# Sums of squares at two changes of layer: vector adds replaced by products with ones

## The chip, the cores and the metric

The kernel runs on one core of a Trainium2 chip. Its time is the device time of one execution in microseconds (us): 3379.16 us, the median of three runs (3367.13, 3379.16 and 3380.83). TensorE (PE) does the matrix products, VectorE (DVE), ScalarE (ACT) and GpSimd (POOL) the elementwise work, SyncE (SP) issues the transfers. Each engine executes its own list of instructions strictly in order, and semaphores tie the lists together.

## What is computed

Two blocks, each two layers deep, over 512 tokens of width 1024, in fp32. The first block has six sublayers (feed-forward, mixer, feed-forward, twice), each between two RMS norms. The second block works on the 512 tokens and on 256 context tokens together: an even layer (a gated recurrence called rwkv, beside a Fourier mix), then an odd layer (retention). What matters here is the frame around every sublayer:

```python
def rmsnorm(x, g):
    xf = x.astype(jnp.float32)
    y = xf * lax.rsqrt(jnp.mean(xf * xf, axis=-1, keepdims=True) + EPS)
    return (y * g.astype(jnp.float32)).astype(x.dtype)

def _sublayer(x, fn, pre_g, post_g, shift, scale, gate, res_w):
    h = _rmsnorm(x, pre_g) * (1.0 + scale[:, None, :]) + shift[:, None, :]
    y = _rmsnorm(fn(h), post_g)
    return x + res_w * (1.0 + gate[:, None, :]) * y
```

So after each sublayer the new x = x + gate*norm(y) is squared, summed over the 1024 features of a token, and the inverse root of that mean scales x for the next sublayer.

## The kernel before

The width lies on the partitions, so x is eight tiles x0 to x7 of 128 features by 512 tokens, and a sum over features is a sum over eight tiles and 128 partitions. `residual` (L389) does the end of a sublayer for one half of 256 tokens: it takes the inverse roots of y (`rstd_bc`, L331: products `st_ps<-ones,yacc`, a square root on ACT, a reciprocal on DVE, and products `bc<-cst,r` that spread the result over all partitions), scales y on DVE, adds it to x on POOL (L402), and squares the new x on ACT. Then there are two ways to the sum. Between the sublayers of block 1 (`boundary`, L416) PE takes for each tile two products `xs<-ones,sq` of one column each, called a pair below; they accumulate over the eight tiles in PSUM. At the two changes of layer (end of block 1 into `even_layer`, and `even_layer` into the odd layer) DVE adds the eight squares into a tile (`sumsq`, L355: `xacc`, `xcacc`, `xkeep`), and only the next layer's `norm_in` (L903) makes products, root, reciprocal and `bc` of it. `norm_in` then computes the split input of the next layer, tile by tile: `hf` on DVE, the high part on ACT, the low part on DVE (`ehh`/`ehl` in the even layer; `oc` for the context, `oh`/`ol` for the tokens in the odd layer).

Every large product is made of three (high by high, high by low, low by high; `acc3`, L270). A weight tile arrives as `raw`, ACT makes its high part `whi`, DVE its low part `wlo`.

In the even layer's recurrence twelve slots follow each other, two per pair of heads. Slots of one kind, called d=0 slots below, carry projections of the context (`ipc`, 24 products of 256 columns) and of the tokens (`ipm`, 24 of 512) as filler beside a chain: DVE solves small triangular systems (`un`), SP moves them through DRAM (`ad<-un`, `blocks<-ad`), DVE transposes them (`tn<-blocks`), and PE and ACT make the block inverse (`p<-tn,am`, `g<-p`, `p<-g,blocks`, `p<-tn,am`, `p<-g,up`). `ipm` has a single PSUM buffer, which ACT frees by reading it (`u<-ipm`). On ACT stand there also the decays (`DC<-L`, `F<-L`, `L<-L`, exponentials of the scans `L` that DVE makes) and a square root `hr<-hst`, which needs another function table and so a table load on each side.

Nothing of the order is written by hand here: a scheduler simulates the program as a whole and writes out one list per engine, so that a change in one place can move instructions elsewhere.

Of the kernel before, what the change touches and what calls it, by code (L numbers as in the profile page):

```python
# [8 lines left out]
F32 = mybir.dt.float32  # L9
F32R = mybir.dt.float32r  # L10
AF = mybir.ActivationFunctionType
# [3 lines left out]
D = 1024  # L15
KD = 8
T = 512
# [131 lines left out]
class K:  # L149
# [236 lines left out]
        self.act(y[o][:, cols], ps[:, cols], AF.Copy)  # L386
        self.sumsq(yacc, ps[:, cols], o == 0, cols)

    def residual(self, x, y, yacc, c0, n, G, xacc=None, last=False):  # L389

        cols = slice(c0, c0 + n)
        bc = self.rstd_bc(yacc, c0, n, 1.0 / D, self.eps6)
        gates = list(zip(self.PEG, self.stats))
        sums = [self.paux("xs", *self.NST) for _ in range(2)] if xacc is None and not last else []
        done = None
        for k in range(KD + 1):
            if k < KD:
                with self.tc.issue_after(done.ins) if done and not self.POOLX else nullcontext():
                    self.stt(y[k][:, cols], y[k][:, cols], G[:, k : k + 1], bc[:, cols])
            if k:  # L400
                new = x[k - 1][:, cols]
                done = (self.nc.vector if last and k % 2 == 0 and (c0 or k > 4) else self.nc.gpsimd).tensor_tensor(out=new, in0=new, in1=y[k - 1][:, cols], op=ALU.add)  # L402
                if xacc is not None:
                    self.sumsq(xacc, new, k == 1, cols)
                elif last:
                    self.nc.sync.dma_start(self.A["out"][k - 1][:, cols], new)
                else:
                    sq = self.tp.tile([128, n], F32, tag=f"sq{n}", name="sq", bufs=self.NSQ)
                    self.act(sq, new, AF.Square)
                    for i, ps in enumerate(sums):  # L410
                        m = self.mm(ps[:, :1], sq[:, 128 * i : 128 * i + 128], self.ones, k == 1, k == KD)
                    gates.append((self.XEG[0] + int(self.XEG[1] * k), m))
        self.pe_gates = [] if last else gates
        return [ps[:, :1] for ps in sums]

    def boundary(self, x, out, G, nxt):  # L416
# [363 lines left out]
    def block1(self, stages, after):  # L780
# [75 lines left out]
        for i, (l, s) in enumerate(order):  # L856
# [25 lines left out]
            if i + 1 < len(order):  # L882
                hs = self.boundary(self.x, out, G, nxt)
            else:
                self.xacc = self.xp.tile([128, 512], F32, tag="xacc", name="xacc")
                for c0, n in self.HALVES:
                    self.residual(self.x, *next(out), c0, n, G(), self.xacc)


    def ada2(self, l, mods):  # L890
# [12 lines left out]
    def norm_in(self, src, acc, g1, shift, hs, c0, halves):  # L903

        for o, n in halves:
            cols, dst = slice(o, o + n), slice(c0 + o, c0 + o + n)
            bc = self.rstd_bc(acc, o, n, 1.0 / D, self.eps6)
            for k in range(KD):
                t = self.t("hf")
                self.stt(t[:, cols], src[k][:, cols], g1[:, k : k + 1], bc[:, cols])  # L910
                hi, lo = hs[k]
                self.act(hi[:, dst], t[:, cols], AF.Identity, bias=shift[:, k : k + 1])
                self.stt(lo[:, dst], t[:, cols], shift[:, k : k + 1], hi.bitcast(F32)[:, dst], ALU.add, ALU.subtract)
# [20 lines left out]
    def even_layer(self):  # L934
# [8 lines left out]
        with tc.tile_pool(name="exc", bufs=1, reuse_waits="tile") as p:  # L943
            self.tp, self.NT = p, 4
            xc = self.load_ctx(p)
            cacc = p.tile([128, TC], F32, name="cacc")
            for k in range(KD):
                self.sumsq(cacc, xc[k], k == 0, slice(0, TC))
            self.norm_in(xc, cacc, g1c, mods["shiftc"], hs, 0, ((0, TC),))
            self.norm_in(self.x, self.xacc, g1l, mods["shiftl"], hs, TC, self.HALVES)  # L950
        xd = self.dp.tile([KD, 128, T], F32, name="xd")
        for k in range(KD):
            nc.sync.dma_start(xd[k], self.x[k])
# [11 lines left out]
        with tc.tile_pool(name="eo", bufs=1, reuse_waits="tile") as p:  # L965
# [4 lines left out]
            y.append(p.tile([128, CT], F32, name="oy"))  # L970
            yc, y = [t[:, :TC] for t in y], [t[:, TC:] for t in y]
            self.out_late(ins, y, yc, yacc, cacc, late, begun)
            self.xcacc = self.xp.tile([128, TC], F32, name="xcacc")
            self.residual(xc, yc, cacc, 0, TC, self.gated("Gc", mods["gatec"], 0, "Gc"), self.xcacc)
            self.xacc = self.xp.tile([128, T], F32, name="xkeep")
            G = self.gated("Gl", mods["gatel"], 0, "G")
            for c0, n in self.HALVES:
                self.residual(self.x, y, yacc, c0, n, G, self.xacc)
        ez_cm.__exit__(None, None, None)
        eh_cm.__exit__(None, None, None)  # L980
        self.xc = xc
# [690 lines left out]
    def odd_layer(self):  # L1672
# [11 lines left out]
        for k in range(KD):  # L1684
            t = self.s(f"oc{k}", F32R)
            hc.append((t[:, :TC], t[:, TC:]))
        self.norm_in(self.xc, self.xcacc, g1c, mods["shiftc"], hc, 0, ((0, TC),))
        self.norm_in(self.x, self.xacc, g1l, mods["shiftl"], hs, 0, self.HALVES)
        con = self.sp.tile([128, OCON.n], F32, name="ocon")
        nc.sync.dma_start(con, A["ocon"])  # L1690
        C = lambda name, n: con[:, OCON.at[name] : OCON.at[name] + n]
# [213 lines left out]
    def program(self, first=True, second=True, stages=6):  # L1905
        nc, tc, A = self.nc, self.tc, self.A
        self.setup()
        with self.phase({"mm": ("mm", 4), "st": ("st", 2), "bc": ("bc", 2)}, (1024, self.NWS[0]), (4, 1), self.NSS):
# [6 lines left out]
            else:  # L1915
# [1 line left out]
                self.flush()  # L1917
                self.open_x()
                self.load_x()
                self.xacc = self.xp.tile([128, 512], F32, tag="xacc", name="xacc")  # L1920
                for k in range(KD):
                    self.sumsq(self.xacc, self.x[k], k == 0, slice(0, T))
        if second:
            with self.phase({"mm": self.INV, "st": ("seq", 1), "bc": ("y", 1)}, (512, self.NWS[1]), None):
                self.even_layer()
# [111 lines left out]
```

## Time and profile before

| | |
|---|---|
| median of three runs | 3379.16 us |
| profiled execution | 3377.71 us |
| its span | 3376.0 us |
| PE busy | 3165.4 us (94%) |
| DVE busy | 1834.4 us (54%) |
| ACT busy | 1189.2 us (35%) |
| POOL busy | 287.1 us (9%) |

The span is what the profile sees of an execution; 1.7 us of the execution's time lie outside it. PE is busy nearly throughout, and the places where it is not are the changes of sublayer and of layer and parts of the recurrence. A busy PE can run at half its clock; the profile gives the granted clock of any stretch (1.00 is 2.4 GHz, 0.50 is 1.2 GHz).

### The profile page before, as it was taken

Reading aid. Unit: us, or ns where it says so; the run is one execution under the profiler, and the core shown is the slowest. Engines: PE = TensorE matmul, PEld = TensorE weight load, DVE = VectorE, ACT = ScalarE, POOL = GpSimd, SP = SyncE. Lnnn points to the kernel's source line nnn. Section 1 sums busy time; section 2 is a strip of 40 time slices with the busy share of each in tenths; the row PEclk is TensorE's granted clock in tenths of the full one; section 3 lists DMA queues with packets and bytes.
Section 4 is the critical chain, followed back from the end, with each engine's and each line's share of the span. In section 5 each row is a group of like instructions: output and inputs, shape, how many; then the busy total and the mean of one; then the engine's idle time right before and its main releaser. Section 6 shows DMA issues by size and latency. Waiting matters only on the chain. (4 is left out here: it accounts for less than half of the span.)

```text
span 3376.0 us, 58396 instructions
## 1 busy us (share of the span) xinstructions
PE 3165.4 (94%) x24530; PEld 2646.8 (78%) x24530; DVE 1834.4 (54%) x3336; ACT 1189.2 (35%) x1925; POOL 287.1 (9%) x285
## 2 busy tenths in 40 slices
PE   5999999999999999999999979999898899869998
PEld 4877887888889888878887868788787778758766
DVE  8554378444425554364667456456655655462554
ACT  4222244432223222344322234233332432242553
POOL 3000020200002000111000010011101111020000
PEclk8999999999999999999999989999999999979999
DMA  6555421144433554332355521211110111222112
GB/s 238 191 181 178 134 82 44 51 145 143 131 96 120 185 176 164 121 102 78 117 182 182 163 87 46 72 31 38 32 30 22 29 58 30 59 67 63 62 39 69
DMA packets 156503, 340.90 MB, mean 101 GB/s; under 512 B 52816, under 2 KB 64848, under 8 KB 156112
## 3 DMA queue, kind: packets, MB, share of 16 engines
q1 hardware_dynamic: 156240, 337.18, 30.8%
q8 instruction: 192, 3.15, 0.4%
q14 instruction: 71, 0.58, 0.1%
HBM read 328.20 MB, written 8.91 MB: 100 GB/s over the span
## 5 line engine op out<-in xcount | busy, mean ns | idle before, releaser
L169 ACT ACTIVATE whi<-raw 128x1024 fp32r<-128x1024 f32 (+2 forms) x451 | 426.0, 947 | 1122.1 <-PE po L174 266.4
L253 DVE TENSOR_TENSOR wlo<-raw,whi 128x1024 fp32r<-128x1024 f32 (+2 forms) x432 | 471.3, 1093 | 539.7 <-ACT whi L169 528.8
L313 DVE CUSTOM_DVE_ANT_0 raw_a<-raw_a,cond 128x1024 f32<-128x1024 f32 x176 | 215.4, 1230 | 339.2 <-DMA raw_a<-in_ada_w_dram 339.1
L174 PE MATMUL pu<-hh,whi 128*128 128x512 f32 (+1 forms) x824 | 317.5, 385 | 5.0 <-ACT whi L169 5.0
L174 PE MATMUL pu<-hh,wlo 128*128 128x512 f32 (+1 forms) x824 | 316.5, 384 | 2.9 <-DVE wlo L253 2.9
L174 PE MATMUL pu<-hl,whi 128*128 128x512 f32 (+1 forms) x824 | 316.2, 384 | 0.0
L174 PE MATMUL pg<-hh,whi 128*128 128x512 f32 (+1 forms) x752 | 293.6, 391 | 22.1 <-ACT hh L169 20.0
L174 PE MATMUL po<-ah,whi 128*128 128x512 f32 (+1 forms) x880 | 309.7, 352 | 3.0 <-ACT sq L169 3.0
L174 PE MATMUL po<-ah,wlo 128*128 128x512 f32 (+1 forms) x880 | 308.7, 351 | 0.0
L174 PE MATMUL po<-al,whi 128*128 128x512 f32 (+1 forms) x880 | 308.0, 350 | 0.0
L174 PE MATMUL pg<-hl,whi 128*128 128x512 f32 (+1 forms) x752 | 291.9, 389 | 5.2 <-DVE hl L188 5.2
L174 PE MATMUL pg<-hh,wlo 128*128 128x512 f32 (+1 forms) x752 | 292.3, 389 | 4.4 <-DVE wlo L253 4.2
L402 POOL TENSOR_TENSOR x<-x,y 128x256 f32<-128x256 f32 x106 | 77.2, 763 | 2107.7 <-DVE y L188 2107.4
L174 PEld LDWEIGHTS pg<-hh,whi 128*128 128x128 f32 x752 | 147.1, 196 | 53.7 <-ACT hh L169 22.2
L174 PEld LDWEIGHTS pu<-hh,whi 128*128 128x128 f32 x824 | 159.0, 193 | 37.4 <-ACT whi L169 5.8
L174 PEld LDWEIGHTS po<-ah,whi 128*128 128x128 f32 x880 | 166.2, 189 | 27.5 <-ACT sq L169 3.8
L174 PEld LDWEIGHTS pu<-hh,wlo 128*128 128x128 f32 x824 | 158.2, 192 | 36.1 <-DVE wlo L253 4.5
L174 PEld LDWEIGHTS po<-al,whi 128*128 128x128 f32 x880 | 166.2, 189 | 23.5
L174 PEld LDWEIGHTS po<-ah,wlo 128*128 128x128 f32 x880 | 166.2, 189 | 23.3
L174 PEld LDWEIGHTS pu<-hl,whi 128*128 128x128 f32 x824 | 158.6, 193 | 31.9
L174 PEld LDWEIGHTS pg<-hh,wlo 128*128 128x128 f32 x752 | 146.3, 195 | 37.5 <-DVE wlo L253 8.4
L174 PEld LDWEIGHTS pg<-hl,whi 128*128 128x128 f32 x752 | 146.0, 194 | 36.0 <-DVE hl L188 6.7
(468 smaller groups left out, 6507.5 us busy)
## 6 DMA issues: line engine op xcount, KB each, us to landing
raw<-in_w_dram SPq DMA_DIRECT2D x232, 512.0 KB, 4.1
raw_a<-in_ada_w_dram SPq DMA_DIRECT2D x176, 512.0 KB, 3.7
raw<-in_ev_in_dram SPq DMA_DIRECT2D x60, 256.0 KB, 2.6
raw<-in_w_dram SPq DMA_DIRECT2D x32, 384.0 KB, 3.6
raw_a<-in_ada_w_dram SPq DMA_DIRECT2D x32, 256.0 KB, 5.6
raw<-in_ab_in_dram SPq DMA_DIRECT2D x16, 512.0 KB, 3.2
raw<-in_ev_out_dram SPq DMA_DIRECT2D x20, 256.0 KB, 2.7
raw<-in_w_dram SPq DMA_DIRECT2D x16, 256.0 KB, 2.6
```

The source lines that it names most:

```text
L169: ins = self.nc.scalar.activation(out=out, in_=in_, func=func, scale=scale, bias=bias)
L174: self.last_mm = self.nc.tensor.matmul(out, lhsT=lhsT, rhs=rhs, start=start, stop=stop)
L253: (self.nc.gpsimd if self.nwt <= self.POOLW else self.nc.vector).tensor_tensor(out=lo, in0=src, in1=hi.bitcast(F32), op=ALU.subtract)
L313: self.nc.vector.tensor_tensor_reduce(out=out, in0=raw, in1=v, scale=1.0, scalar=0.0, op0=ALU.mult, op1=ALU.add, accum_out=dst[:, o : o + 1])
L402: done = (self.nc.vector if last and k % 2 == 0 and (c0 or k > 4) else self.nc.gpsimd).tensor_tensor(out=new, in0=new, in1=y[k - 1][:, col ...
```

## The change

At both changes of layer `residual` now makes the sums the way `boundary` does, with pairs on PE, and it keeps the inverse roots themselves: ACT takes each square root straight from PSUM into a column of a small tile (`xrs`, four columns of 128 tokens each; `xcrs`, two columns for the context), DVE inverts them in place, and `norm_in` only spreads them (`bc<-cst,xrs`).

```diff
-    def residual(self, x, y, yacc, c0, n, G, xacc=None, last=False):
+    def residual(self, x, y, yacc, c0, n, G, keep=None, last=False):
...
-        sums = [self.paux("xs", *self.NST) for _ in range(2)] if xacc is None and not last else []
+        sums = [] if last else [self.paux("xs", *(self.NST if keep is None else self.NMM)) for _ in range(2)]
...
-                if xacc is not None:
-                    self.sumsq(xacc, new, k == 1, cols)
-                elif last:
+                if last:
                     self.nc.sync.dma_start(self.A["out"][k - 1][:, cols], new)
                 else:
                     sq = self.tp.tile([128, n], F32, tag=f"sq{n}", name="sq", bufs=self.NSQ)
                     self.act(sq, new, AF.Square)
                     for i, ps in enumerate(sums):
                         m = self.mm(ps[:, :1], sq[:, 128 * i : 128 * i + 128], self.ones, k == 1, k == KD)
-                    gates.append((self.XEG[0] + int(self.XEG[1] * k), m))
+                    if keep is None:
+                        gates.append((self.XEG[0] + int(self.XEG[1] * k), m))
         self.pe_gates = [] if last else gates
+        if keep is not None:
+            for i, ps in enumerate(sums):
+                self.act(keep[:, i : i + 1], ps[:, :1], AF.Sqrt, scale=1.0 / D, bias=self.eps6)
+            self.nc.vector.reciprocal(out=keep, in_=keep)
...
-                self.xacc = self.xp.tile([128, 512], F32, tag="xacc", name="xacc")
+                self.xrs = self.xp.tile([128, 4], F32, name="xrs")
                 for c0, n in self.HALVES:
-                    self.residual(self.x, *next(out), c0, n, G(), self.xacc)
+                    self.residual(self.x, *next(out), c0, n, G(), self.xrs[:, c0 // 128 : (c0 + n) // 128])
...
-            bc = self.rstd_bc(acc, o, n, 1.0 / D, self.eps6)
+            if isinstance(acc, tuple):
+                bc = self.paux("bc", *self.NBC)
+                for c in range(o, o + n, 128):
+                    self.mm(bc[:, c : c + 128], acc[0][:, c // 128 : c // 128 + 1].to_broadcast([128, 128]), self.con("ident", 128))
+            else:
+                bc = self.rstd_bc(acc, o, n, 1.0 / D, self.eps6)
...
-            self.xcacc = self.xp.tile([128, TC], F32, name="xcacc")
-            self.residual(xc, yc, cacc, 0, TC, self.gated("Gc", mods["gatec"], 0, "Gc"), self.xcacc)
-            self.xacc = self.xp.tile([128, T], F32, name="xkeep")
+            self.xcrs = self.xp.tile([128, 2], F32, name="xcrs")
+            self.residual(xc, yc, cacc, 0, TC, self.gated("Gc", mods["gatec"], 0, "Gc"), self.xcrs)
+            self.xrs = self.xp.tile([128, 4], F32, name="xrs")
             G = self.gated("Gl", mods["gatel"], 0, "G")
             for c0, n in self.HALVES:
-                self.residual(self.x, y, yacc, c0, n, G, self.xacc)
+                self.residual(self.x, y, yacc, c0, n, G, self.xrs[:, c0 // 128 : (c0 + n) // 128])
```

The lists of the engines differ at the two changes of layer and in three slots of the recurrence between them.

First place, the first change of layer, PE, before: the products `po` of the last feed-forward's second half, while the first half's residual runs on the other engines (numbers tell tiles of one name apart).

```order
L174 MATMUL po<-ah_13417,whi 128x256
L174 MATMUL po<-al_13418,whi 128x256
L174 MATMUL po<-ah_13417,wlo 128x256
L174 MATMUL po<-ah_13498,whi 128x256
L174 MATMUL po<-al_13499,whi 128x256
L174 MATMUL po<-ah_13498,wlo 128x256
```

The same place after the change:

```order
L174 MATMUL po<-ah_13417,whi 128x256
L174 MATMUL xs<-ones,sq 128x1 x2
L174 MATMUL po<-al_13418,whi 128x256
L174 MATMUL po<-ah_13417,wlo 128x256
L174 MATMUL xs<-ones,sq 128x1 x2
L174 MATMUL po<-ah_13498,whi 128x256
L174 MATMUL po<-al_13499,whi 128x256
L174 MATMUL xs<-ones,sq 128x1 x2
L174 MATMUL po<-ah_13498,wlo 128x256
L174 MATMUL po<-ah_13577,whi 128x256
```

Eight pairs of `xs` (each `x2`) now stand between these `po` products; the pairs of the second half follow after the last `po`.

Second place, the second change of layer, PE, before: from the norms of y to the first product of the odd layer (`pv`).

```order
L174 MATMUL st_ps<-ones,yacc 128x1 x2
L174 MATMUL bc<-cst,r 128x128 x2
L174 MATMUL st_ps<-ones,yacc 128x1 x2
L174 MATMUL bc<-cst,r 128x128 x4
L174 MATMUL st_ps<-ones,xcacc 128x1 x2
L174 MATMUL bc<-cst,r 128x128 x2
L174 MATMUL st_ps<-ones,xkeep 128x1 x2
L174 MATMUL bc<-cst,r 128x128 x2
L174 MATMUL st_ps<-ones,xkeep 128x1 x2
L174 MATMUL bc<-cst,r 128x128 x2
L174 MATMUL pv<-whi,oh_26715 128x512
```

After the change, the same stretch:

```order
L174 MATMUL st_ps<-ones,yacc 128x1 x2
L174 MATMUL bc<-cst,r 128x128 x2
L174 MATMUL st_ps<-ones,yacc 128x1 x2
L174 MATMUL xs<-ones,sq 128x1 x6
L174 MATMUL bc<-cst,r 128x128 x2
L174 MATMUL xs<-ones,sq 128x1 x14
L174 MATMUL bc<-cst,r 128x128 x2
L174 MATMUL xs<-ones,sq 128x1 x28
L174 MATMUL bc<-cst,xcrs 128x128 x2
L174 MATMUL bc<-cst,xrs 128x128 x4
L174 MATMUL pv<-whi,oh_26778 128x512
```

The `st_ps` products on `xcacc` and `xkeep` are gone, 24 pairs stand in three groups between the `bc` products of y, and all `bc` of the next layer stand behind the last pair.

The same place on DVE, before (`oy` is y, scaled; `hf` opens the next layer's norm):

```order
L188 SCALAR_TENSOR_TENSOR oy<-oy,Gl,bc 128x256 x2
L183 TENSOR_TENSOR xkeep<-xkeep,sq 128x256
L188 SCALAR_TENSOR_TENSOR oy<-oy,Gl,bc 128x256 x6
L183 TENSOR_TENSOR xkeep<-xkeep,sq 128x256 x5
L348 RECIPROCAL r<-r 128x2
L183 TENSOR_TENSOR xkeep<-xkeep,sq 128x256 x4
L188 SCALAR_TENSOR_TENSOR hf<-xc_26342,g1c,bc 128x256
L188 SCALAR_TENSOR_TENSOR hf<-xc_26343,g1c,bc 128x256
L188 SCALAR_TENSOR_TENSOR hf<-xc_26344,g1c,bc 128x256
```

After the change:

```order
L348 RECIPROCAL r<-r 128x2
L188 SCALAR_TENSOR_TENSOR oy<-oy,Gl,bc 128x256 x8
L416 RECIPROCAL xcrs<-xcrs 128x2
L188 SCALAR_TENSOR_TENSOR oy<-oy,Gl,bc 128x256 x8
L416 RECIPROCAL xrs<-xrs 128x2 x2
L188 SCALAR_TENSOR_TENSOR hf<-xc_26360,g1c,bc 128x256
L188 SCALAR_TENSOR_TENSOR hf<-xc_26361,g1c,bc 128x256
```

The 21 adds are gone, and the context's first `hf` stands behind the reciprocals of all six columns.

Third place, a d=0 slot of the recurrence (the second of the three that differ), ACT, before:

```order
L169 ACTIVATE kd<-alm,a0h 128x512
L169 ACTIVATE whi<-raw 128x512
L169 ACTIVATE u<-ipm 128x512
L169 ACT_TABLE_LOAD
L169 ACTIVATE hr<-hst 128x12
L169 ACT_TABLE_LOAD
L169 ACTIVATE DC<-L 128x12
L169 ACTIVATE F<-L 128x12x64
L169 ACTIVATE r<-u,omu 128x768
L169 ACTIVATE rt<-hr 128x768
L169 ACTIVATE L<-L 128x768
L169 ACTIVATE whi<-raw 128x512 x2
```

After the change:

```order
L169 ACTIVATE kd<-alm,a0h 128x512
L169 ACTIVATE DC<-L 128x12
L169 ACTIVATE F<-L 128x12x64
L169 ACT_TABLE_LOAD
L169 ACTIVATE hr<-hst 128x12
L169 ACT_TABLE_LOAD
L169 ACTIVATE L<-L 128x768
L169 ACTIVATE whi<-raw 128x512
L169 ACTIVATE u<-ipm 128x512
```

The weight's `whi` and `u<-ipm`, which stood ahead of both table loads, now stand behind them and behind the exponentials `DC`, `F` and `L`. In the same slot DVE now finishes `un` before it starts the scans `L`, and its transposes `tn<-blocks` move ahead of the work on `r`; PE still runs fourteen `ipc`, fourteen `ipm` and the spreads `hbc`/`hbm` first, but takes `p<-tn,am` ahead of the other ten `ipc` and ten `ipm` instead of behind them, and `p<-g,blocks` behind nineteen of these.

## Rows read from the trace of the kernel before

**Rows 1.** The page, busy time of each engine:

```profile
PE 3165.4 (94%) x24530; PEld 2646.8 (78%) x24530; DVE 1834.4 (54%) x3336; ACT 1189.2 (35%) x1925; POOL 287.1 (9%) x285
```

**Rows 2.** Windows: length, busy time of PE, PEld, DVE, ACT, POOL; then the clock:

```profile
2340.40:2407.10 66.70, 65.19 (x1117) 57.73 (x1119) 45.36 (x103) 28.72 (x48) 8.60 (x9) 1.00 0.14 38
2474.00:2541.20 67.20, 62.41 (x1117) 55.21 (x1115) 43.87 (x105) 26.28 (x43) 8.10 (x9) 0.95 0.12 30
...
1997.00:2011.00 14.00, 0.00 (x0) 0.00 (x0) 9.49 (x21) 6.67 (x16) 6.37 (x9) 0.50 0.78 258
...
2967.00:2996.00 29.00, 8.97 (x38) 8.06 (x36) 27.73 (x66) 14.65 (x37) 20.20 (x24) 0.50 0.18 73
```

**Rows 3.** Timeline of PE, a boundary inside block 1: start, duration, instruction:

```profile
425.10 0.50 PE L174 MATMUL xs<-ones,sq 128*128 128x1 f32 x4
...
425.67 0.28 PE L174 MATMUL po<-al,whi 128*128 128x256 f32 x1
425.78 0.50 PE L174 MATMUL xs<-ones,sq 128*128 128x1 f32 x4
```

**Rows 4.** Timeline of all engines, first change of layer, second half of tokens:

```profile
1997.15 0.42 ACT L169 ACTIVATE xacc<-x 128x256 f32<-128x256 f32 x1 [2.68 <-POOL x L402]
...
2004.10 3.65 SPq L928 DMA_DIRECT2D xc<-in_ctx_dram  x8
...
2012.39 1.01 PE L174 MATMUL st_ps<-ones,xacc 128*128 128x1 f32 x4 [0.35 <-ACT r L169]
2013.27 1.20 PE L174 MATMUL bc<-cst,r 128*128 128x128 f32 x4
```

**Rows 5.** Timeline of all engines, second change of layer:

```profile
2970.64 1.19 PE L174 MATMUL bc<-cst,r 128*128 128x128 f32 x4 [2.76 <-DVE r L348]
...
2973.90 14.18 POOL L402 TENSOR_TENSOR x<-x,oy 128x256 f32<-128x256 f32 x16
...
2988.81 1.65 DVE L188 SCALAR_TENSOR_TENSOR hf<-xc,g1c,bc 128x256 f32<-128x256 f32 x4
...
3005.03 0.51 PE L174 MATMUL pc<-whi,oc 128*128 128x512 f32 x1 [0.93 <-DVE hf L188]
```

**Rows 6.** Timeline of POOL at a boundary inside block 1, beside no DVE adds:

```profile
445.00 5.56 POOL L402 TENSOR_TENSOR x<-x,y 128x256 f32<-128x256 f32 x8 [1.11 <-DVE y L188]
```

**Rows 7.** Windows of PE alone at a boundary inside block 1: length, busy, clock:

```profile
449.30:450.50 1.20, 1.20 (x14) 1.00 0.00 0
...
451.60:452.66 1.06, 1.06 (x8) 0.77 0.02 8
```

**Rows 8.** Timeline of all engines in the second slot that differs:

```profile
2504.25 1.26 DVE L1388 TENSOR_TENSOR_SCAN L<-ec,sig 128x256 f32<-128x256 f32 x2
2504.45 0.59 ACT L169 ACTIVATE u<-ipm 128x512 f32<-128x512 f32 x1
2505.05 1.28 ACT L169 ACT_TABLE_LOAD   x1
2505.36 0.40 PE L174 MATMUL ipm<-ehh,whi 128*128 128x512 f32 x1
...
2507.97 0.83 ACT L169 ACTIVATE F<-L 128x768 f32<-128x768 f32 x1
...
2511.00 0.62 ACT L169 ACTIVATE whi<-raw 128x512 fp32r<-128x512 f32 x1
...
2515.80 1.67 PE L174 MATMUL p<-tn,am 64*64 64x64 f32 x48 [2.16 <-DVE tn L1538]
2518.42 3.00 PE L174 MATMUL p<-g,blocks 64*64 64x64 f32 x48 [0.95 <-ACT g L169]
...
2524.15 1.61 PE L174 MATMUL p<-g,up 64*64 64x64 f32 x48
```

**Rows 9.** Timeline of PE in the last d=0 slot, where ACT's order is late already:

```profile
2758.53 0.58 PE L174 MATMUL eoc<-eyh,whi 128*128 128x256 f32 x1 [3.37 <-ACT eyh L169]
...
2762.46 0.63 PE L174 MATMUL eom<-eyh,wlo 128*128 128x512 f32 x1
```

## What the change does to the time

> **What bounds the kernel now.** I read the page's engine table first: PE is busy for 94% of the span [rows 1], so an edit pays or costs where PE waits or where it adds work to PE. The windows by stage say where it waits. In the two stages that the change is about PE does little: at the first change of layer it does nothing in 14 us while DVE, ACT and transfers work, at the second it is busy for 8.97 of 29 us, both at half its clock (0.50, which is 1.2 GHz) [rows 2]. There the bound is a chain: square, sum, root, norm of the next layer. The third view is the timeline at these places and in the three slots of the recurrence that the order changes; in the windows of the first two of them PE idles 1.5 and 4.8 us [rows 2].
>
> **First change of layer.** On the first half of tokens eight pairs of one-column products now stand among products that PE runs back to back. The trace has such pairs inside block 1: from one pair's start to the next is 0.68 us with two `po` products between, and a `po` alone takes 0.11 (425.67 to 425.78) [rows 3]. So a pair costs 0.68 - 2 x 0.11 = 0.46 us, and eight cost 3.6 us. Nothing hides them, because the second half's y waits for the last `po`. At the half clock a pair costs 0.88 us (2012.39 to 2013.27, four records as here) [rows 4], so the bounds are 0 (PE waits for something else) and 7.0.
>
> On the second half the context load waits for the last reader of the squares: before, DVE's last add, and the load was issued at 2004.10; now it is PE's last pair. The first square ends at 1997.57 [rows 4] and eight pairs at 0.88 end at 2004.6: +0.6 us. `st_ps<-ones,xacc` no longer stands between the context's reciprocal and its `bc` on PE, which frees part of its 0.88 us: -0.7. The seven adds of this half that DVE drops saved nothing else: PE idles there anyway. Sum of the place: 3.6 + 0.6 - 0.7 = +3.5 us; with the bounds of the pair -0.1 to +6.9.
>
> **Second change of layer.** DVE loses 21 adds, PE gains 24 pairs, and `bc` of the next layer stands behind the last of them, as does the context's first `hf` on DVE (behind the reciprocals). Before, that `hf` started at 2988.81, after POOL's 16 adds, which ended at 2988.08 [rows 5]. Now three pairs push the first `bc` of y from 2970.64 [rows 5] to about 2971.6. From there PE has two `bc` (2.1 us), 21 pairs and one more `bc` (1.1) in one row: at 0.88 a pair 2971.6 + 2.1 + 18.5 + 1.1 = 2993.3. POOL is done earlier than that and no longer counts. `hf` starts 4.5 us late. Two adds and two reciprocals that stood between the context's `hf` and the token `hf` that frees the buffer for `pc` are gone (about 0.4 us an add, as the `hf` of the same size: 1.65 for four [rows 5]; with the reciprocals about 1.3). Before, PE runs without a gap from `pc` at 3005.03 [rows 5], so what counts is when it gets there: +3 us. If each pair cost 0.46, the row would end near 2984 and POOL would decide again.
>
> POOL itself should be faster here. Eight adds took 5.56 us (0.70 each) beside no DVE adds [rows 6], and 16 took 14.18 (0.89 each) among them [rows 5]. The Trainium skill has a rule for that in "SBUF — State Buffer", section "Who interferes with whom": a VectorE instruction with both inputs in SBUF contends with GpSimd instructions that read SBUF, and the loser waits for the whole instruction. The rows agree (0.89 against 0.70), and by the rule alone this place would gain about 3 us instead of losing 3.
>
> The bounds are -1 (pairs at 0.46: the second half's y is scaled from about 2980, eight adds at 0.70 end near 2986, the last square, pair, root and `bc` bring `hf` to 2988.8, and the 1.3 us remain) and +4.5 (nothing of the 1.3 counts). I take +3, since all of 2967 to 2996 ran at the half clock before.
>
> The page "TensorE: Matmul & The Clock Gate" of the Trainium skill says in Part 1, on the clock gate, that sustained activity lifts the clock; by it 21 pairs in a row would lift it and the place would come to -1. The trace speaks against that: in a row of nothing but such pairs the granted clock went down, from 1.00 at 449.3 to a mean of 0.77 from 451.60 to 452.66, while the records show PE busy all the time [rows 7].
>
> **The three slots.** I expect most of the cost here, though the edit is elsewhere. In the second of them ACT freed `ipm` at 2505.04 and PE started the next `ipm` at 2505.36, without a wait [rows 8]. Now `u<-ipm` stands behind `DC`, `F`, two table loads, `hr`, `L` and `whi`, and these wait for DVE's scans, which end at 2505.51 [rows 8] (the last adds of `un` now come ahead of them; the wait for `sig` that stood there goes). From 2505.6: `DC` and `F` 1.0, a table load 1.3, `hr` 0.2, a table load 1.3, `L` as long as `F` 0.8, `whi` 0.5, `u<-ipm` 0.6, in all 5.7: 2511.3. PE runs out of `ipc` before that, since their second weight tile is that same `whi`, so `ipm` starts 6.0 us late, on a cold clock. How long it stays cold I take from the last d=0 slot, which has ACT's late order already: there PE waited 3.37 us and ran 512 columns in 0.63 us still 3.9 us after it resumed [rows 9], where 0.40 is usual [rows 8]. That makes another 2 us.
>
> Against this stand the new order's gains. DVE finishes `un` ahead of the scans, so the blocks are there before PE asks for them, and the 2.16 us that PE waited at `p<-tn,am` go. Fourteen `ipm` (14 x 0.23 us) and the spreads (1.3) behind 2511.3, with the 2 us, give `p<-tn,am` at 2517.8 (before 2515.80). Then 1.6 for it and 3.3 for the filler: `p<-g,blocks` at 2522.7 (before 2518.42). It took 3.00 us on a cold clock before, the last `p` products 1.61 [rows 8]; warm now, two products of 1.6 with 0.8 of waits for DVE and ACT bring `p<-g,up` to 2526.7 against 2524.15: +2.6 us. The rest of the slot is one chain from there and shifts. The third slot repeats the pattern: +2.6.
>
> The first slot differs: its 24 `ipc` all stand ahead of `ipm`, so 1.2 us of the hole are filled, but PE had only 1.5 us of waits to give back [rows 2]. 6.0 - 1.2 + 0.7 of cold clock - 1.5 = +4. Sum of the slots: +9 us. Bounds: at full clock throughout the same sums give 0.6, 0.6 and 2, so +3, and if the scans come a microsecond earlier about 0; if the hole and the cold clock count in full, 8 + 8 + 5.5 = +21.
>
> **Sum.** 3.5 + 3 + 9 = +15.5 us on the profiled execution's 3377.7 (a span of 3376.0 and 1.7 us around it): 3393.2. The median of the runs is 1.5 us above that execution and the three runs differ by 14 us, so I say 3393 for the median too. Against 3379.2 that is +0.4%. About 0.5%, or 16.9 us, is what a measurement of this kernel can tell from no change; the forecast is no change, with most of its weight above zero.
>
> **Rivals.**
> - The slots give the hole back. For: PE idled 4.8 us in the second slot's window [rows 2] and ran `p<-g,blocks` cold, so there is slack. Against: on PE `p<-tn,am` stands behind `ipm` and cannot pass it. Slots 0 to +3, so about 3.5 + 3 + 1.5 = +8: 3386.
> - The row of pairs warms PE up, by the rule on the clock: -1 at the second change of layer, so 3.5 - 1 + 9 = +11.5: 3389. Against it stand the 0.77 of rows 7.
> - Slower. The hole is not regained because the `p` products behind it run cold as they did before (3.00 for 1.61 [rows 8]): another 1.4 us for each of the two that I take as warm, so 5.4 in the second and third slot and 6 in the first, 17 us. With 6.5 us from the two changes of layer that is +23: 3401. It decides as soon as the slots cost more than 10.4 us together. The waits of 3.37 us in the last d=0 slot [rows 9] speak for it; that PE now has filler between these products speaks against it.
> - A real gain: the two waits of the second slot (2.16 and 0.95 us [rows 8]) go in all three and nothing takes their place, the pairs are hidden, POOL's 3 us count. 0 - 3 - 9 = -12: 3366. The place of `u<-ipm` is against it.
>
> **How the numbers follow.** Forecast 0.48, slots give back 0.20, warm pairs 0.07, slower 0.20, gain 0.05. The forecast's own range is 3387 to 3400; some three tenths of it lie beyond 0.5%. So slower has 0.20 + 0.13 = 0.33, faster 0.04 (most of the last rival), the rest 0.63. The range reaches from 3376, where the lower bounds of the three places meet (-0.1 - 1 + 0), to 3405, beyond the slower case.
>
> **What would show it.** `po` with pairs between them at the first change of layer, one pair for about 0.46 us. At the second, one row of pairs at 0.85 to 0.88, clock 0.50, the context's `hf` 4 to 5 us late against PE's last `eoc`, and POOL's 16 adds in about 11 to 12 us. In each of the three slots, PE idle behind `ipc` for some 4 to 6 us with ACT's `whi` or `u` as the releaser, and no more wait for `tn`. The prediction is wrong if PE finds no hole there, if the pairs run at 0.46, or if a slot loses less than a microsecond in spite of the hole.

## The result and the profile after

The changed kernel takes 3403.61 us (median of 5 runs, 3398.13 to 3405.52), the kernel before 3379.08 us beside it on the same chip (3367.13 to 3380.83). The ratio is 1.0079, with a 95% interval of 1.0062 to 1.0096: 24.5 us slower by the medians, where the forecast was 14 us and no change. The profiled execution of after took 3403.09 us, with a span of 3400.8.

The page's engine table of after answers to [rows 1]:

```profile
PE 3201.2 (94%) x24670; PEld 2674.7 (79%) x24670; DVE 1814.4 (53%) x3301; ACT 1194.0 (35%) x1930; POOL 282.8 (8%) x285
```

PE has 140 instructions more and is busy 35.8 us longer, DVE 35 instructions less and 20.0 us shorter. To find the time I took one event that both traces have (a product, a transfer), subtracted its start before from its start after, and read from the place where this difference grows. Two executions with the same lists drift by 2 to 3 us against each other over the recurrence, so sizes below come from short stretches, or from kernels that differ in one part alone.

**First change of layer.** The timeline of PE, after (start, duration, instruction, [idle ahead <-releaser]):

```profile
1980.72 0.50 PE L174 MATMUL st_ps<-ones,yacc 128*128 128x1 f32 x4
...
1986.72 0.50 PE L174 MATMUL xs<-ones,sq 128*128 128x1 f32 x4
...
1999.07 0.60 PE L174 MATMUL st_ps<-ones,yacc 128*128 128x1 f32 x4 [1.21 <-DVE yacc L183]
...
2003.34 6.99 PE L174 MATMUL xs<-ones,sq 128*128 128x1 f32 x32 [1.89 <-ACT sq L169]
2018.21 0.98 PE L174 MATMUL st_ps<-ones,cacc 128*128 128x1 f32 x4 [7.88 <-DVE cacc L183]
2019.84 1.19 PE L174 MATMUL bc<-cst,r 128*128 128x128 f32 x4 [0.64 <-DVE r L348]
```

The same products before:

```profile
1978.78 0.50 PE L174 MATMUL st_ps<-ones,yacc 128*128 128x1 f32 x4
...
1993.56 0.61 PE L174 MATMUL st_ps<-ones,yacc 128*128 128x1 f32 x4 [1.21 <-DVE yacc L183]
...
2011.03 1.01 PE L174 MATMUL st_ps<-ones,cacc 128*128 128x1 f32 x4 [15.30 <-DVE cacc L183]
```

From the first half's `st_ps<-ones,yacc` to the second half's passed 18.35 us (1980.72 to 1999.07), before 14.78 (1978.78 to 1993.56): eight pairs cost 3.57 us. The second half's pairs are one row of 6.99 us, 0.87 a pair, and the context load behind them is issued at 2010.41 (before 2004.10, [rows 4]), another 0.8 us late. The sum of the context (`st_ps<-ones,cacc`) then comes 0.87 us later still behind its load (7.80 us, before 6.93); why its last piece took longer stays open. From there to the context's `bc` passed 1.63 us, before 2.24 (2011.03 to 2013.27, [rows 4]), 0.61 less, since no `st_ps<-ones,xacc` stands between them. Together that is 4.6 us at this `bc`; 1.9 us more had been lost ahead of anything that the change touches.

**First slot of the recurrence.** The shift against before is 6.4 us at the transfer `un<-ad` of the first slot (2101.33 against 2094.90) and 13.1 at that of the second (2216.53 against 2203.44). The lists of PE and ACT are the same here; only DVE's differs. The timeline of DVE, before:

```profile
2092.25 0.69 DVE L183 TENSOR_TENSOR gk<-pg,ec 128x512 f32<-128x512 f32 x1 [3.45 <-PE pg L174]
2094.85 0.69 DVE L183 TENSOR_TENSOR gk<-pg,ec 128x512 f32<-128x512 f32 x1 [1.91 <-PE pg L174]
2096.76 0.17 DVE L183 TENSOR_TENSOR tmp<-un 96x14 f32<-96x14 f32 x1 [1.22 <-DMA un<-ad]
...
2098.43 0.68 DVE L183 TENSOR_TENSOR gk<-pg,ec 128x512 f32<-128x512 f32 x1
```

The same place after:

```profile
2103.20 0.17 DVE L183 TENSOR_TENSOR tmp<-un 96x14 f32<-96x14 f32 x1 [6.94 <-DMA un<-ad]
...
2103.50 0.67 DVE L183 TENSOR_TENSOR gk<-pg,ec 128x512 f32<-128x512 f32 x1
...
2107.53 0.68 DVE L183 TENSOR_TENSOR gk<-pg,ec 128x512 f32<-128x512 f32 x1
...
2111.00 0.68 DVE L183 TENSOR_TENSOR gk<-pg,ec 128x512 f32<-128x512 f32 x1
```

The three `gk`, two of which stood ahead of the transfer's wait, now stand behind it and among the adds of `un`, the third behind the last of them. PE takes them in order for `pw<-vt,gk`, as its timeline shows, before:

```profile
2098.26 1.15 PE L174 MATMUL pw<-vt,gk 64*64 64x64 f32 x32
...
2100.25 0.68 PE L174 MATMUL pw<-vt,gk 64*64 64x64 f32 x16
...
2106.62 1.15 PE L174 MATMUL pt<-cst,ar 64*64 64x64 f32 x32
```

and after:

```profile
2105.73 0.68 PE L174 MATMUL pw<-vt,gk 64*64 64x64 f32 x16
...
2108.27 0.68 PE L174 MATMUL pw<-vt,gk 64*64 64x64 f32 x16 [1.86 <-DVE gk L183]
...
2111.73 1.12 PE L174 MATMUL pw<-vt,gk 64*64 64x64 f32 x16 [1.50 <-DVE gk L183]
2113.37 0.63 PE L174 MATMUL ipm<-ehl,whi 128*128 128x512 f32 x1
...
2120.00 1.15 PE L174 MATMUL pt<-cst,ar 64*64 64x64 f32 x32
```

The first `pw` starts 7.47 us later than before (2105.73, before 2098.26), so that much PE had lost already; the last one starts 11.48 us later and takes 1.12 instead of 0.68 us, the `ipm` behind it takes 0.63 instead of 0.40, and the `pt` behind these starts 13.38 us later. On PE this place alone costs 5.9 us in this execution. The prediction does not speak of it, and the section on the change names three slots of the recurrence with new lists, where there are four.

**The three later slots.** The windows of after that answer to the first two of [rows 2] (length, busy PE, PEld, DVE, ACT, POOL, clock):

```profile
2352.52:2423.09 70.57, 68.13 (x1117) 59.56 (x1119) 45.71 (x103) 29.17 (x48) 8.96 (x9) 0.98 0.13 36
2489.65:2560.23 70.58, 64.34 (x1117) 55.21 (x1115) 43.96 (x105) 26.64 (x43) 8.33 (x9) 0.95 0.11 28
```

These slots are 3.9 and 3.4 us longer; the third is 1.8 us longer (2625.91 to 2694.71, before 2607.00 to 2674.00). The hole is where the prediction has it. The timeline of the first and of the second of the three, the second answering to [rows 8]:

```profile
2382.32 0.58 PE L174 MATMUL ipc<-ehh,whi 128*128 128x256 f32 x1 [2.12 <-ACT whi L169]
...
2525.81 0.61 ACT L169 ACTIVATE whi<-raw 128x512 fp32r<-128x512 f32 x1
2526.33 0.58 ACT L169 ACTIVATE u<-ipm 128x512 f32<-128x512 f32 x1
2526.48 0.58 PE L174 MATMUL ipc<-ehh,whi 128*128 128x256 f32 x1 [4.28 <-ACT whi L169]
...
2527.07 0.68 PE L174 MATMUL ipm<-ehh,whi 128*128 128x512 f32 x1
...
2661.04 0.39 PE L174 MATMUL ipc<-ehh,whi 128*128 128x256 f32 x1 [2.09 <-ACT whi L169]
```

PE idles 4.28 us behind `ipc` in the second slot, and ACT's `whi` releases it; the last line is the same place in the third slot. The first and the third hole, 2.12 and 2.09 us, are shorter than the 4 to 6 us that the prediction names. The first `ipm` of the second slot comes at 2527.07, before at 2505.36 [rows 8]; less the 15.65 us by which the slot starts late (its window, 2489.65 against 2474.00), it is 6.1 us late, where the prediction has 6.0.

**Second change of layer.** The timeline of PE, after, answering to [rows 5]:

```profile
2994.53 5.97 PE L174 MATMUL xs<-ones,sq 128*128 128x1 f32 x28
...
3001.36 11.95 PE L174 MATMUL xs<-ones,sq 128*128 128x1 f32 x56
...
3013.17 1.20 PE L174 MATMUL bc<-cst,xcrs 128*128 128x128 f32 x4
```

Its window (length, busy PE, PEld, DVE, ACT, POOL, clock) shows PE busy throughout at half its clock:

```profile
2994.00:3014.00 20.00, 20.00 (x96) 20.00 (x96) 6.95 (x19) 8.99 (x25) 12.29 (x18) 0.50 0.01 2
```

A pair takes 0.85 us (11.95 / 14), and the context's first `hf` starts at 3014.47, right behind `bc`. What the place costs shows between two products that both kernels have, before

```profile
2962.75 1.02 PE L174 MATMUL st_ps<-ones,cacc 128*128 128x1 f32 x4 [5.12 <-DVE cacc L183]
...
3025.31 0.63 PE L174 MATMUL pc<-whi,oc 128*128 128x512 f32 x2
```

and after:

```profile
2984.66 1.01 PE L174 MATMUL st_ps<-ones,cacc 128*128 128x1 f32 x4 [5.13 <-DVE cacc L183]
...
3050.19 0.63 PE L174 MATMUL pc<-whi,oc 128*128 128x512 f32 x2
```

The first is 21.91 us late, the second 24.88: 3.0 us. The context's first `hf` is 3.8 us late by the same measure (25.66 less 21.91). The group of POOL's adds there (busy, mean ns) reads

```profile
L402 POOL TENSOR_TENSOR x<-x,oy 128x256 f32<-128x256 f32 x16 | 11.0, 728 | 1.4 <-DVE oy L188 1.3
```

That is 0.69 us an add (11.0 / 16) where it was 0.89 (14.18 / 16, [rows 5]); by the mean of the single records, which overlap a little, it is 728 ns where it was 920. The page "SBUF — State Buffer" of the Trainium skill, section "Who interferes with whom", describes such contention, of a VectorE instruction with two inputs in SBUF with a GpSimd instruction that reads SBUF; the trace agrees, 0.89 with DVE's adds beside POOL's and 0.69 without. The faster adds brought nothing, since the pairs are the last to end.

### The profile page after: what moved, and what is told of

It reads as the page before. It is cut to its first block, busy times and chain, and to the rows that moved or that the text cites. A ratio compares the mean times of both kernels' runs of the same rounds, so it can differ in the third digit from the quotient of the medians.

```text
span 3400.8 us, 58633 instructions
## 1 busy us (share of the span) xinstructions
PE 3201.2 (94%) x24670; PEld 2674.7 (79%) x24670; DVE 1814.4 (53%) x3301; ACT 1194.0 (35%) x1930; POOL 282.8 (8%) x285
```

## Experiments

Theory A, formed on the traces: the edit itself costs little (the two changes of layer), and most of the loss comes from the lists that the scheduler wrote elsewhere, a part of it in the first slot. Rival B: the lists don't matter, the pairs cost more than their own time. The prediction as it stands is the third: three slots, nothing in the first. All ratios are against the kernel before, run beside the kernel; in brackets stands the 95% interval.

**The two halves of the edit: sums alone, lists alone.** In one kernel the sums are those of after, and in the recurrence every engine's list is held in the order that it had before; in the other the sums are those of before and the lists those of after. Holding a list adds an order and no wait, and by itself it costs nothing: a run below holds every list, with only the three `gk` products moved, and lands at a ratio of 1.0000. The lines that hold one list:

```diff
+        for a, b in zip(row, row[1:]):
+            self.tc.add_manual_dep(ins[b], ins[a].name, NoSync)
```

New sums, old lists:

> The new sums at both changes of layer, but every engine's list in the whole recurrence held in the order it had before. Theory A (orders): of the 24.5 us lost, about 6 come from VectorE's list in the first slot, where the `gk` products of the masks went behind the first adds of `un`, about 9 from the three slots with ScalarE's new list, and the rest, 9, from the sums themselves. Then the run gives back 15 us and lands near 3388. Theory B (sums): the recurrence only passes on what the changes of layer cost, and the lists cost nothing: 3403. The prediction on record had no loss in the first slot: it would see 9 given back, 3394. PE should show no waits for `gk` any more.

3383.95 us, ratio 1.0026 (1.0016 to 1.0035): +8.8 us. (Differences are the ratio's excess times some 3378 us, here and below; after's is 26.7 by that, 24.5 by the medians.)

Old sums, new lists:

> The kernel before, sums on VectorE as they were, but every engine's list in the recurrence in the order of the changed kernel. Theory A: 15 us slower with not one instruction more, about 3394, 6 of them between the first `ad` reads and the end of `un`'s adds. Theory B: no change, 3379. By the prediction on record +9, about 3388.

3392.66 us, 1.0051 (1.0039 to 1.0064): +17.2 us. The two add up to 26.0, after's loss, and two thirds of it are in the lists. B falls.

**The first slot.** After, with DVE's list of the first slot as before:

```diff
-tmp un gk tmp un ... tmp gk un ... wlo tmp un gk
+gk gk tmp un tmp un tmp wlo un gk tmp un ... tmp un
```

> The changed kernel with VectorE's old list in the first slot of the recurrence alone (the `gk` products ahead of `un`'s first add); the three later slots stay as changed. Theory A: 6 us faster than the changed kernel, about 3397.5, and no idle PE ahead of `pw<-vt,gk`. Rival: PE waited there for something that comes late anyway (the transfer `un<-ad`, the half-clock stretch), so the wait moves and no more than 2 us come back: 3402 or more.

3396.44 us, 1.0058 (1.0044 to 1.0072): 7 us of after's loss are back, though this interval and after's (1.0062 to 1.0096) still overlap. The converse, the kernel before with this one list of after, is clear of no change:

> The kernel before, with one thing changed: VectorE's list in the first slot of the recurrence is that of the changed kernel (`gk`'s three products stand behind, in the middle of and at the end of `un`'s adds). Every other list is held as before. By the theory that this list alone costs the part that the prediction missed: +6 to +7 us, about 3383, with PE idle twice ahead of `pw<-vt,gk` and half the clock behind it. Rival: it only hurts together with the later changes of layer: no change.

3383.79 us, 1.0020 (1.0011 to 1.0028): +6.8 us by the ratio, 7.05 by the medians (before: 3376.74). PE's two stalls are in its timeline:

```profile
2104.35 1.12 PE L178 MATMUL pw<-vt,gk 64*64 64x64 f32 x16 [2.86 <-DVE gk L187]
...
2107.81 1.12 PE L178 MATMUL pw<-vt,gk 64*64 64x64 f32 x16 [0.76 <-DVE gk L187]
```

Is it the wait for the transfer, or the place among `un`'s adds? Here, on the kernel before, all three `gk` stand behind the transfer as in after, but directly behind `un`'s first pair, with only one `wlo` between the second and the third:

```diff
-gk gk tmp un tmp un tmp wlo un gk tmp un ... tmp un
+tmp un gk gk wlo gk tmp un ... tmp un
```

> As the run with the first slot's new list, but `gk`'s three products follow each other directly behind `un`'s first multiply and add, so they still wait for the transfer `un<-ad`, but no longer for the other adds of `un`. If the transfer is what costs, the loss stays at 6 to 7 us. If the cost is that the second and the third product stand deep among `un`'s adds, PE finds them ready (`pw` came at 2105.73, and all three would be done near 2106) and the loss is under 1 us: about 3377.

3376.86 us, 1.0000 (0.9991 to 1.0009). The timeline of DVE shows the transfer waited for as long as in after:

```profile
2094.49 0.17 DVE L187 TENSOR_TENSOR tmp<-un 96x14 f32<-96x14 f32 x1 [7.73 <-DMA un<-ad]
...
2094.79 1.27 DVE L187 TENSOR_TENSOR gk<-pg,ec 128x512 f32<-128x512 f32 x2
...
2096.58 0.68 DVE L187 TENSOR_TENSOR gk<-pg,ec 128x512 f32<-128x512 f32 x1
```

DVE idles 7.73 us there and the kernel is no slower. The loss is the second and third `gk`, deep among the adds.

**The three later slots.** The kernel before, with after's lists in these three slots alone:

> The kernel before with the changed kernel's lists in the three later slots alone; the first slot keeps the old list. By the step of the prediction on these slots: +9 us, with holes of PE ahead of `ipm`. By subtraction of the two runs with all new lists (17) and with the first slot's (7): +10. If the lists only add up when all of them are new, it is less than 5.

3387.15 us, 1.0026 (1.0014 to 1.0038): +8.8 us (4.7 to 12.8), the prediction's +9.

**The second change of layer alone.** The first one keeps its adds:

```diff
-                    self.residual(self.x, *next(out), c0, n, G(), self.xrs[:, c0 // 128 : (c0 + n) // 128])
+                    self.residual(self.x, *next(out), c0, n, G(), self.xacc)
```

> New sums at the second change of layer alone; the recurrence keeps its old lists without being held. Theory: PE's row of pairs at the half clock is the bound there, +3 to +4 us, about 3383. Rival on the POOL side (its 16 adds are faster without VectorE's adds beside them, and the row keeps pace with them): -1 to 0, 3378 to 3379.

3380.84 us, 1.0013 (1.0001 to 1.0024): +4.4 us (0.3 to 8), with 3.0 us in the trace of after above. In the recurrence its lists are those of before, so by subtraction the first change costs the rest of the 8.8 us, 4.4; the trace of after has 4.6.

**What a pair costs.** On the new sums with the old lists, the eight pairs of the first half are doubled (the root's scale is halved, so the sum is the same):

```diff
+                        for j in range(self.times):
+                            m = self.mm(ps[:, :1], sq[:, 128 * i : 128 * i + 128], self.ones, k == 1 and j == 0, k == KD and j == self.times - 1)
```

> New sums with the recurrence's lists held as before, and at the first change of layer each of the eight pairs of the first half of tokens done twice (the sums double, the root takes half). Theory: these pairs stand among products that PE runs back to back, and eight more cost 8 x 0.46 = 3.7 us: about 12 us above the kernel before, where the same kernel with single pairs was 8.7 above. Rival: PE has slack there and they are hidden: still 8.7 above. Second rival: at the half clock's 0.88 a pair, 7 us more.

3395.71 us, 1.0058 (1.0045 to 1.0070): +19.6 us, that is some 11 more for eight pairs (5 to 16 by the two intervals), not 3.7. The timeline of PE and the windows (length, busy PE, PEld, DVE, ACT, POOL, clock) show why:

```profile
1982.95 10.03 PE L179 MATMUL xs<-ones,sq 128*128 128x1 f32 x64
...
1985.00:1987.00 2.00, 2.00 (x20) 2.00 (x19) 0.00 (x0) 1.04 (x3) 0.00 (x0) 0.98 0.00 0
1987.00:1989.00 2.00, 2.00 (x12) 2.00 (x11) 0.00 (x0) 0.12 (x1) 0.00 (x0) 0.50 0.00 0
...
1997.00:1999.00 2.00, 2.00 (x18) 2.00 (x17) 1.62 (x3) 0.91 (x2) 0.00 (x0) 0.96 0.03 8
```

All sixteen pairs (64 records, four a pair) stand in one row of 10.03 us. PE is never idle, yet some 4 us into this row the granted clock falls from 0.98 to 0.50; the rest of the row and the `po` behind it run at the half clock until 1997. From the first half's `st_ps<-ones,yacc` to the second half's pass 26.66 us here (1976.96 to 2003.62), 8.3 more than in after. So I thought that the row was the cause, and spread the doubled pairs, two `po` between any two:

```diff
+                        self.queue_ins(m.ins, po[52 + 2 * g - 1])
+                    self.queue_ins(po[52 + 2 * g], self.pairs_in[2 * g + 1].ins)
```

> As the run with the doubled pairs, with the same sixteen pairs and the same arithmetic, but PE's list is made to have two `po` products between any two pairs; there, thirty-two one-column products stood in a row and the granted clock fell to 0.50 behind them. If the row is what made eight more pairs cost some 10 us, the clock stays at 1.00 here, eight more cost 8 x 0.46 = 3.7 us, and the run lands 10 to 12 us above the kernel before instead of 19. If each pair costs 0.85 wherever it stands, it stays at 17 to 19 above.

3397.37 us, 1.0056 (1.0034 to 1.0077): +19 us again. The expectation that the clock stays up fell; the windows of this kernel:

```profile
1988.00:1990.00 2.00, 2.00 (x20) 2.00 (x20) 0.00 (x0) 0.72 (x2) 0.00 (x0) 1.00 0.00 0
1990.00:1992.00 2.00, 2.00 (x13) 2.00 (x12) 0.37 (x1) 1.72 (x4) 0.00 (x0) 0.58 0.00 0
```

The clock falls here too, some 5 us behind the first pair (1985.22). So standing in one row is not what brings it down; what of the pairs does stays open. Sixteen are not needed either. In the profiled execution of after the clock stays at 1.00 at this place, but in that of the run with the new sums and the old lists, with the same eight pairs at the same distances, it falls from 1.00 to 0.50 behind the last of them:

```profile
1986.00:1988.00 2.00, 2.00 (x14) 2.00 (x15) 0.84 (x3) 1.61 (x6) 0.00 (x0) 0.72 0.00 0
1988.00:1990.00 2.00, 2.00 (x11) 2.00 (x10) 1.04 (x2) 0.23 (x1) 0.00 (x0) 0.50 0.16 40
```

There the way from `st_ps<-ones,yacc` to `st_ps<-ones,yacc` takes 19.84 us (1975.14 to 1994.98), so the eight pairs cost 5.1 us in place of 3.57. That the price of the first change came out as forecast in the trace of after is in part luck of that execution.

**A gain elsewhere? The last d=0 slot.** There ACT's order is late in the kernel before as well [rows 9]. In this kernel the two engines' lists are held in another order there (ACT above, DVE below):

```diff
-eyh ... sig sig kd
+sig sig kd ... eyh
-eyl ... L (scans)
+L (scans) ... eyl
```

> A version that may beat both: the kernel before, with its old sums and lists, but in the last d=0 slot ScalarE does `sig` (twice) and `kd` ahead of the split of `eyh`, for which it stood 3.67 us waiting on a transfer, and VectorE does its scans ahead of `eyl` and of `un`'s last adds. The root `hr` then comes some 4 us earlier and the 2.90 us that PE waits at `hbc<-cst,rt` go, with part of the cold clock behind them: -3 to -5 us, about 3373. Rival: PE meets the same hole one step later, at the `p` products: 0 to -1.

3377.54 us, 0.9998 (0.9989 to 1.0008): no gain. The first expectation fell: `hbc<-cst,rt` no longer waits, but PE now waits 2.42 us at `p<-tn,am` instead. The hole moved and did not close.

**An earlier load of the context.** In the kernel before, the context's load at the first change of layer waits for the last reader of the squares, whose memory it takes, and stands behind copies of x in SP's queue. Two memory pools of the first phase change places, so that it no longer shares it, and the load is issued ahead of the copies:

```diff
+        if sp:
+            self.sp = pool("sp")
...
-        if sp:
-            self.sp = pool("sp")
...
+            with self.tc.issue_after(self.last_ctx.ins):
-            nc.sync.dma_start(xd[k], self.x[k])
+                nc.sync.dma_start(xd[k], self.x[k])
```

> Old sums, old lists in the recurrence, but the pools of the first layer lie in another order, so that the context load at the first change of layer no longer waits for the last reader of the squares' buffers, and the queue does it ahead of the copies of x. What bounds that place would then be ScalarE's row of squares, x's eight ahead of the context's eight: the last one ends 3.5 us behind x's last (2003.15), near 2006.6, where it was 2010.5. -4 us, about 3373. Rival: VectorE's norm is the bound behind it and only passes part of it on: -1.

3346.20 us, 0.9904 (0.9888 to 0.9921): -32 us. With the context's squares and adds put ahead of those of x's second half as well (`square` and `add` are the first ones of that half):

```diff
+            self.queue(square, self.squares[-1])
+            self.queue(add, self.adds[-1])
```

> As the run with the early context load, and ScalarE and VectorE also do the context's squares and adds ahead of the last ones of x's second half. The context's first `hf` on VectorE then stands only behind x's last add, near 2004.5, where it was 2014.50: -8 to -10 us, about 3368, faster than both kernels. Rival: the norm that starts earlier meets the transfers of the weights, or PE's `ipc` waits for x's norm all the same: -4, as the run without the new order.

3341.53 us, 0.9891 (0.9874 to 0.9908): -37 us, the fastest kernel here. PE's two `bc` in its timeline, that of x's second half and that of the context:

```profile
1969.46 0.71 PE L178 MATMUL bc<-cst,r 128*128 128x128 f32 x4 [0.55 <-DVE r L355]
...
1981.83 1.20 PE L178 MATMUL bc<-cst,r 128*128 128x128 f32 x4
```

At the place itself the first kernel gains the 3.7 us that were expected (from the second half's `bc` to the context's: 14.83 us, before 18.55), the second 6.2 (12.37 us). The other 30 come from elsewhere. The order of the two pools alone:

> The kernel before with nothing changed but the order in which two pools of the first phase are laid out in SBUF (the large tiles' pool ahead of the squares' pool); every engine's list in the recurrence is held, ACT, DVE and PE have the same lists as before, and the context load still stands behind most copies of x in its queue. The run with this order and the early context load was 32 us faster than before, of which the trace puts 4 at the change of layer and some 23 into the blocks ahead of it, where a 512-column product starts every 0.226 us in place of 0.233. If placement alone does that: -25 to -29 us, about 3350 to 3355. If the early load does it by way of its transfers: 0 to -2.

3347.55 us, 0.9910 (0.9896 to 0.9924): -30 us with the same lists of ACT, DVE and PE. A window of 100 us inside block 1, before:

```profile
700.00:800.00 100.00, 100.00 (x430) 80.46 (x430) 42.19 (x53) 29.09 (x36) 0.00 (x0) 1.00 0.40 137
```

and with the pools exchanged:

```profile
700.00:800.00 100.00, 100.00 (x443) 82.81 (x442) 42.95 (x55) 29.43 (x37) 0.00 (x0) 1.00 0.44 146
```

PE is busy all the time at clock 1.00 in both, but 443 products start instead of 430: one every 0.226 us, not 0.233. Ahead of this window the lists are the same and only the addresses of the tiles differ. Why they matter was not tried. The change itself does not touch this rate: in the same window of after 430 products start, as before.

Last, the sums of after with the old lists on top of the exchanged pools and the early load:

> The changed kernel's sums at both changes of layer, with the old lists in the recurrence, the other pool order and the early context load. It tells how much of the first change's loss was the load waiting behind PE's pairs: with the load freed, the second half's pairs lie beside the context's squares and cost nothing. Then the new sums cost only the first half's pairs (3.6 to 5) and the second change (3 to 4): 7 to 9 us above the run with the old sums and the same pools (3346), about 3354, still far under the kernel before. Rival: PE's row of pairs at the half clock (7 us) is then what the context's sum waits for: 3356 to 3358.

3351.99 us, 0.9921 (0.9907 to 0.9934): 5.7 us more by the ratios than the same kernel with the adds, 0.9904 (0.9888 to 0.9921). The two ran at different times on different chips and their intervals overlap, so that a loss on this base is likely but not shown; a gain is not in sight.

## Why the prediction was wrong

- **First change of layer, +3.5 predicted.** Right in mechanism, a little low: in the trace of after 3.57 us for the eight pairs against 3.6 from [rows 3], 0.8 for the load against 0.6, and -0.61 against the -0.7 for `st_ps<-ones,xacc`. The 0.87 us that the context's sum came later behind its load are not in the forecast; the place costs 4.6 in the trace and 4.4 by the runs. That a pair among the `po` could take the clock down with it, as it did in one execution (5.1 us for the eight), is not in the forecast either.
- **Second change of layer, +3.** Right: pairs at 0.85 at the half clock, POOL's 16 adds at 11.0 us in sum (11 to 12 predicted) and off the chain, `bc` behind the last pair. The context's `hf` is 3.8 us late, not 4 to 5. The place costs 3.0 us in the trace, and +4.4 us (0.3 to 8) when run by itself.
- **The three slots, +9.** Right: 8.8 us when run by themselves, with holes behind `ipc` and ACT's `whi` as the releaser, and `ipm` 6.1 us late in the second slot. The holes of the first and third slot were half as long as said (2.12 and 2.09 us), and of the division (4 + 2.6 + 2.6) the second slot was too low and the third too high: the windows show 3.9, 3.4 and 1.8.
- **The step that failed: "Sum of the slots: +9 us".** It counts three slots, as the section on the change does. DVE's list differs in a fourth, the first of the recurrence, where PE's and ACT's are the same, so that slots looked for by PE and ACT miss it. It costs 6.8 us when run alone (3.7 to 9.5), and with it the sum passes the 16.9 us below which the prediction speaks of no change. The prediction's 15.5 and these 6.8 make 22.3; the four parts, 4.4 + 6.8 + 8.8 + 4.4, make 24.4, where after lost 26.7 by the ratio (21 to 32) and 24.5 by the medians. The first of the four is by subtraction, and each is known to some 3 or 4 us.
- **Its sums.** 8 x 0.46 is 3.7 and not 3.6, 2004.6 is 0.5 behind 2004.10 and not 0.6, three tenths of 0.48 are 0.14 and not 0.13, and with the 1.5 us between the profiled execution and the median 3393.2 would be 3394.7. None of it changes the forecast.
- **The rivals.** "Slower" came closest in size (3401), by luck: its 17 us were to come from three slots whose products ran cold, and the 17.2 us measured for the lists are those of four slots. That the row of pairs would warm PE up did not happen (0.50). The three slots gave no more back than the forecast has, and nothing was gained.

## What to carry to other kernels

Where a scheduler writes the lists, compare them on every engine over the whole program before pricing an edit: here 17 of some 25 us lie where the code was not touched, and a list that differs on one engine alone cost 7. On an engine that takes its list in order, a product that another engine needs piece by piece must not be strewn through a chain of short instructions; here a wait of 7.7 us ahead of it was free, its place among the adds was not. The small instructions themselves were priced well from rows of the same instructions elsewhere in the trace, as long as the clock was the same in both places.

## What the runs showed of the hardware

- PE was busy in every window while its granted clock fell from 1.00 to 0.50, where pairs of one-column products stood among 256-column ones: with sixteen pairs in one row some 4 us into the row, with sixteen spread some 5 us behind the first, and with eight in one execution (new sums, old lists) but not in that of after. Against the way in after, which has eight pairs at clock 1.00, the sixteen cost 8.3 us more in a row and 9.8 us more spread (28.17 us between the two `st_ps<-ones,yacc`), where the first eight cost 3.57. A row of 14 pairs behind a half-clock stretch stayed at 0.50 for all of its 11.95 us.
- Where tiles lie in memory set how fast 512-column products follow each other, at the same clock and with PE busy throughout: 0.233 or 0.226 us, 30 us of 3377 for the kernel. That is as much as the whole change cost.
- POOL's adds with two inputs in SBUF took 0.69 us each (11.0 / 16) without DVE's adds beside them, and 0.89 (14.18 / 16) among them.
